# Transposing feed-forward features with VectorE blocks and SBUF-to-SBUF transfers in place of TensorE

## The chip, the cores and the metric

The kernel runs on one core of one Trainium2 chip. The metric is device microseconds for one execution. The profile is of one such execution; in it PE is TensorE's matmuls, PEld its weight loads, DVE is VectorE, ACT is ScalarE, SP is SyncE, whose queue issues nearly all transfers. L404 is line 404 of the kernel before.

## The reference

The computation is one layer of an encoder on 256 tokens of width 2048, all in float32. The change touches only the channel sub-layer, a SwiGLU feed-forward network with 5632 inner features:

```python
h = h + rms_norm(mixed, g_mix_post[i])
fn = rms_norm(h, g_ffn_pre[i])
ff = (jax.nn.silu(fn @ w_ffn_gate[i]) * (fn @ w_ffn_up[i])) @ w_ffn_down[i]
h = h + rms_norm(ff, g_ffn_post[i])
```

Before it comes a mixing sub-layer (input projection, neighbourhood attention, a gated recurrence, output projection), after it a per-layer embedding gated by one more 2048x2048 projection.

## The kernel before

Tokens are in two tiles `t` of 128 (`NT` = 2). Every large product reads its weight matrix in tiles of 256x512 numbers (512 KB): SP loads one into `wr` (L337), ACT copies it, rounded to a shorter format, into `wh` (L360), DVE writes what the rounding left off into `wl` (L370), and TensorE forms three products per 128 rows and per token tile (L404 to L406): high by high, high by low, low by high. One weight tile is thus 12 matmuls of 512 columns. There are four `wr` buffers and four pairs `wh`/`wl`.

The inner features come in eleven pieces of 512, `f` = 0 to 10, in three parts: pieces 0 to 3, 4 to 7 and 8 to 10. For each piece, 8 weight tiles of `w_ffn_gate` and 8 of `w_ffn_up` are multiplied. `gate_post` puts the gate half through SiLU on ACT into `mid` (L1200); `up_post` multiplies the up half into it on DVE (L1212). The result `e` has tokens on the partitions. The down product needs the features there, so `up_post` has TensorE transpose `e` in 128x128 blocks, four blocks at a time, into a PSUM bank `tr` (`transposed`, L260), and `split` turns `tr` into a high half (ACT, L241) and a low half (DVE, L243), named `mid0h` and `mid0l` in the first part. After the pieces of a part come its 512-wide column blocks of the down product, 32 weight tiles of `w_ffn_down` (24 in the last part), which read those halves.

The order on every engine is fixed when the kernel is built. A planner keeps an estimated clock for ACT, DVE, PE and the transfers. Small tasks are generators: each `yield act(...)`, `yield dve(...)`, `yield dma(...)` names an engine and an estimated cost, and the planner places it among the rest. TensorE's main order of matmuls comes from the sequence of segments; other tasks are fitted around it. Each engine, and SP's queue, then works through its list strictly in order.

Of the kernel before, what the change touches and what calls it, by code (L numbers as in the profile page):

```python
# [10 lines left out]
F32 = mybir.dt.float32  # L11
# [5 lines left out]
P = 128  # L17
S = 256
NT = S // P
# [8 lines left out]
N = 512  # L28
# [20 lines left out]
W_BUFS = 4  # L49
R_BUFS = 4  # L50
SM_BUFS = 4
# [5 lines left out]
class Event:  # L57


    t = None  # L60
# [124 lines left out]
def act(n, tables=COPY, take=None, give=None):  # L185
    return ("act", 0.15 + 0.00082 * n, tables, take, give)


def dve(n, take=None, give=None):
    return ("dve", 0.08 + 0.00104 * n, None, take, give)  # L190


def pe(cost, take=None, give=None):
    return ("pe", cost, None, take, give)


def dma(kb, take=None):
    return ("dma", kb / 340.0, None, take, None)
# [3 lines left out]
def layer(ctx: ExitStack, tc: tile.TileContext, a: dict, out: bass.AP):  # L202
    nc = tc.nc
# [1 line left out]
    wp = ctx.enter_context(tc.tile_pool(name="wp", bufs=W_BUFS))  # L205
    at = ctx.enter_context(tc.tile_pool(name="at", bufs=1))
    ps = ctx.enter_context(tc.tile_pool(name="ps", bufs=4, space=bass.MemoryType.PSUM))
    plan = Plan(wr=R_BUFS, w=W_BUFS, sm=SM_BUFS, ev=1, mid=2, bt=2)

    def f32(t):  # L210
        return t.bitcast(F32)

    def bank(name):
        return ps.tile([P, 2, S], F32, tag="sm", name=name, bufs=SM_BUFS)
# [23 lines left out]
    def split(hi, lo, src, n, give=None):  # L238

        yield act(n)  # L240
        nc.scalar.copy(hi, src)  # L241
        yield dve(n, give=give)
        nc.vector.tensor_tensor(out=lo, in0=src, in1=f32(hi), op=ALU.subtract)  # L243
# [9 lines left out]
    def transposed(e, b0):  # L253

        yield pe(0.44, take="sm")
        tr = bank("tr")
        for b in range(2):
            for t in range(NT):
                sl = slice((b0 + b) * P, (b0 + b + 1) * P)
                nc.tensor.transpose(tr[:, b, t * P : (t + 1) * P], e[:, t, sl], ident)  # L260
        return tr
# [13 lines left out]
    def done(event):  # L275
        event.t = plan.now
# [35 lines left out]
    def seg(chunk, w, n0, lhs, ks, first=True, last=True, after=None):  # L312
        s = (chunk, lhs, ks, first, last, after, len(tiles))
        for k, _ in ks:
            tiles.append((w, k, n0))
        segs.append(s)
# [658 lines left out]
    KS = [(k, k) for k in range(0, KD, 2)]  # L975
# [13 lines left out]
    t2 = {}  # L989

    def open_p2():
        for e in mixT.ev:
            plan.reach(e)
        p1_ctx.close()
        rs = ctx.enter_context(tc.tile_pool(name="rs", bufs=1))
        t2["pool"] = rs
        for n in ("h", "mg", "ple"):
            t2[n] = rs.tile([P, NT, D], F32, name=n)
        t2["pTh"] = rs.tile([P, 2, S], F32R, name="pTh")
        t2["pTl"] = rs.tile([P, 2, S], F32R, name="pTl")  # L1000
        t2["pw"] = rs.tile([P, 2, S], F32, name="pw")
        plan.add(load_p2(), plan.clk["pe"])

    pT = Act(2)
# [9 lines left out]
    def load_p2():  # L1014
        yield from load_gain("g_mix_post")
        done(ev_gain["mix"])
        yield dma(256)
        here = Event()
        nc.sync.dma_start(t2["pw"], a["pT"].rearrange("(k p) s -> p k s", p=P))
        done(here)  # L1020
        for t in range(NT):
            yield dma(1024)
            nc.sync.dma_start(t2["h"][:, t, :], a["x"][t * P : (t + 1) * P, :])
        done(ev_h)
        yield here
        yield from split(t2["pTh"], t2["pTl"], t2["pw"], 2 * S)
        pT.blocks(t2["pTh"], t2["pTl"], 0, 2)
        pT.pair(0)
# [131 lines left out]
    hF = Act()  # L1160
    rstd_f, ev_rf = small("rstd_f"), Event()

    def sub_post(sub, c, add=False, after=None):
        def post(ch):
            if c == 3:
                plan.add(after(), plan.now)
            yield from sub.chunk(c, ch, add)
        return post

    def after_mix():  # L1170
# [3 lines left out]
    A_KS = [(k, k) for k in range(0, 8, 2)]  # L1174
    ch = [
        Chunk(sub_post(mix, c, after=after_mix), None if c else open_p2) for c in range(4)
    ]
    for c in range(2):
# [14 lines left out]
    def gate_post(f):  # L1193
        def post(ch):
            yield ev_rf
            for t in range(NT):
                yield act(N, SILU, take=None if t else "mid")
                if t == 0:
                    es[f] = t2["pool"].tile([P, NT, N], F32, tag="mid", name="mid", bufs=2)
                nc.scalar.activation(  # L1200
                    es[f][:, t, :], ch.accs[t], AF.Silu, scale=rstd_f[:, t : t + 1]
                )
            done(ch.free)
        return post

    def up_post(f, mid, kk0, g):
        def post(ch):
            yield g.free
            e = es.pop(f)
            for t in range(NT):  # L1210
                yield dve(N)
                nc.vector.scalar_tensor_tensor(  # L1212
                    out=e[:, t, :], in0=ch.accs[t], scalar=rstd_f[:, t : t + 1], in1=e[:, t, :],
                    op0=ALU.mult, op1=ALU.mult,
                )
            done(ch.free)
            for b in range(0, 4, 2):
                tr = yield from transposed(e, b)
                if b == 2:
                    plan.free["mid"].append(plan.now)  # L1220
                kk = kk0 + b
                i, j = divmod(kk, 8)
                hi, lo = mid.tiles(i)
                yield from split(hi[:, j : j + 2, :], lo[:, j : j + 2, :], tr, 2 * S, give="sm")
                mid.pair(kk)
        return post

# [12 lines left out]
    def down_post(part, c):  # L1240
        def post(ch):
            sl = slice(c * N, (c + 1) * N)
            mg = t2["mg"]
            for t in range(NT):
                if part == 0:
                    yield act(N)
                    nc.scalar.copy(mg[:, t, sl], ch.accs[t])
                else:
                    yield dve(N)
                    nc.vector.tensor_tensor(  # L1250
                        out=mg[:, t, sl], in0=ch.accs[t], in1=mg[:, t, sl], op=ALU.add
                    )
            done(ch.free)
        return post
# [5 lines left out]
    for part, (f0, f1) in enumerate(parts):  # L1260
        mid = Mid(f"mid{part}")
        for f in range(f0, f1):
            g = Chunk(gate_post(f))
            seg(g, "w_ffn_gate", f * N, hF, KS)
            seg(Chunk(up_post(f, mid, (f - f0) * 4, g)), "w_ffn_up", f * N, hF, KS)
        for c in range(4):
            last = part == len(parts) - 1
            post = sub_post(ffn, c, True, after_ffn) if last else down_post(part, c)
            seg(Chunk(post), "w_ffn_down", c * N, mid,
                [(f0 * 4 + k, k) for k in range(0, (f1 - f0) * 4, 2)],  # L1270
                after=(lambda: load_sqrt()) if last and c == 3 else None)
# [13 lines left out]
    def load_sqrt():  # L1285
        plan.add(preload(AF.Sqrt, SQRT), plan.clk["pe"])
# [155 lines left out]
```

## Time and profile before

| | |
|---|---|
| median of 3 runs | 1195.0 us (1194.61 to 1195.26) |
| profiled execution, whole time | 1195.0 us |
| its span, first to last instruction | 1193.2 us |
| mean granted TensorE clock | 0.997 |
| PE / DVE / ACT busy share | 99% / 58% / 53% |
| share of the 16 DMA engines used by SP's queue | 59.3% |

A busy share says how full an engine is on average, not whether it sets the end; for that one reads the chain that ended last. A group's line gives `output<-inputs`, the shape, how often it ran, its busy time and its mean, and what it waited for. A DMA line gives the time from issue to landing, so its wait in the queue is in it. Matmuls overlap: one is recorded with about 390 ns, while the next starts some 227 ns after it, so what a matmul costs is read from starts.

### The profile page before, as it was taken

To read this page: it belongs to the slowest core of one execution; us is meant where nothing else is said; L and a number is where in the kernel's file an instruction comes from. 1 tells how busy PE (TensorE), PEld (TensorE's weight loads), DVE (VectorE), ACT (ScalarE), POOL (GpSimd) and SP (SyncE) were. 2 spreads that over 40 slices of the span, in tenths; PEclk is the share of its full clock that TensorE was granted. 3 is DMA by queue.
4 is the path that set the end of the run, shared out by engine and by line. 5 is a ranking of instruction groups with operands and counts; after the bars stand their busy time and mean duration, and the time that the engine had idled before them with its cause. 6 is when DMAs were issued, how large, how long until landed. Compare 5 with 4: busy or idle time off the path is not lost.

```text
span 1193.2 us, 14281 instructions
## 1 busy us (share of the span) xinstructions
PE 1180.8 (99%) x5396; PEld 978.0 (82%) x5396; DVE 697.7 (58%) x822; ACT 632.8 (53%) x836; POOL 1.2 (0%) x11
## 2 busy tenths in 40 slices
PE   9999999999999999999999999999999999999996
PEld 6888888888888888888888888888888888888885
DVE  6667967877557544544444544545454544657664
ACT  6777787866457444444444444444334444446753
POOL 0000000000000000000000000000000000000000
PEclk9999999999999999999999999999999999999998
DMA  9665555465856565565556565555665556565661
GB/s 339 228 207 191 171 186 189 153 192 188 301 192 197 193 194 190 186 191 190 194 195 194 182 197 185 189 196 181 194 193 194 191 181 194 175 209 177 221 220 71
DMA packets 69653, 233.01 MB, mean 195 GB/s; under 512 B 7376, under 2 KB 14160, under 8 KB 68944
## 3 DMA queue, kind: packets, MB, share of 16 engines
q1 hardware_dynamic: 69440, 232.03, 59.3%
q8 instruction: 42, 0.69, 0.2%
q14 instruction: 27, 0.22, 0.1%
q10 hardware_dynamic: 144, 0.08, 0.0%
HBM read 229.98 MB, written 2.10 MB: 195 GB/s over the span
## 4 chain that ended last, share of the span: by engine, by line
PE 98%; DMA 1%; DVE 1%; ACT 0%; SPq 0%; DVEq 0%; issue 0%
PE acc L406 31%; PE acc L405 31%; PE acc L404 31%; PE tr L260 2%; DMA wr<-in_w_in 1%; PE pg L265 0%; PE pg L266 0%; PE pg L264 0%; DVE wl L370 0%; DVE h L1328 0%; PE po L265 0%; PE po L266 0%; PE po L264 0%; PE sc L265 0%; PE sc L266 0%; PE sc L264 0%
## 5 line engine op out<-in xcount | busy, mean ns | idle before, releaser
L370 DVE TENSOR_TENSOR wl<-wr,wh 128x1024 fp32r<-128x1024 f32 x406 | 494.6, 1223 | 382.7 <-ACT wh L360 382.4
L360 ACT CAST wh<-wr 128x1024 fp32r<-128x1024 f32 x406 | 426.2, 1052 | 469.8 <-PE acc L406 450.5
L404 PE MATMUL acc<-wh,hT_mix_hi 128*128 128x512 f32 x704 | 275.8, 392 | 0.0
L406 PE MATMUL acc<-wh,hT_mix_lo 128*128 128x512 f32 x704 | 274.3, 390 | 0.3 <-DVE hT_mix_lo L249 0.3
L405 PE MATMUL acc<-wl,hT_mix_hi 128*128 128x512 f32 x704 | 274.0, 389 | 0.0
L406 PEld LDWEIGHTS acc<-wh,hT_mix_lo 128*128 128x128 f32 x704 | 132.2, 188 | 28.4 <-DVE hT_mix_lo L249 0.9
L405 PEld LDWEIGHTS acc<-wl,hT_mix_hi 128*128 128x128 f32 x704 | 132.3, 188 | 26.8
L404 PEld LDWEIGHTS acc<-wh,hT_mix_hi 128*128 128x128 f32 x704 | 132.2, 188 | 26.7
L404 PE MATMUL acc<-wh,hT_hi 128*128 128x512 f32 x312 | 123.8, 397 | 0.0
L405 PE MATMUL acc<-wl,hT_hi 128*128 128x512 f32 x312 | 121.9, 391 | 0.4 <-DVE wl L370 0.4
L406 PE MATMUL acc<-wh,hT_lo 128*128 128x512 f32 x312 | 121.9, 391 | 0.0
L405 PEld LDWEIGHTS acc<-wl,hT_hi 128*128 128x128 f32 x312 | 58.7, 188 | 12.8 <-DVE wl L370 1.5
L406 PEld LDWEIGHTS acc<-wh,hT_lo 128*128 128x128 f32 x312 | 58.6, 188 | 12.4
L404 PEld LDWEIGHTS acc<-wh,hT_hi 128*128 128x128 f32 x312 | 58.7, 188 | 11.4 <-ACT hT_hi L247 0.2
L404 PE MATMUL acc<-wh,mid0h 128*128 128x512 f32 x128 | 50.0, 390 | 0.0
L404 PE MATMUL acc<-wh,mid1h 128*128 128x512 f32 x128 | 50.0, 390 | 0.0
L406 PE MATMUL acc<-wh,mid0l 128*128 128x512 f32 x128 | 49.8, 389 | 0.0
L406 PE MATMUL acc<-wh,mid1l 128*128 128x512 f32 x128 | 49.8, 389 | 0.0
L405 PE MATMUL acc<-wl,mid0h 128*128 128x512 f32 x128 | 49.8, 389 | 0.0
L405 PE MATMUL acc<-wl,mid1h 128*128 128x512 f32 x128 | 49.8, 389 | 0.0
L404 PE MATMUL acc<-wh,hT_ffn_hi 128*128 128x512 f32 x112 | 44.2, 394 | 0.0
L406 PE MATMUL acc<-wh,hT_ffn_lo 128*128 128x512 f32 x112 | 43.7, 390 | 0.0
(236 smaller groups left out, 1330.3 us busy)
## 6 DMA issues: line engine op xcount, KB each, us to landing
wr<-in_w_ffn_gate SPq DMA_DIRECT2D x88, 512.0 KB, 4.1
wr<-in_w_ffn_up SPq DMA_DIRECT2D x88, 512.0 KB, 4.1
wr<-in_w_ffn_down SPq DMA_DIRECT2D x88, 512.0 KB, 4.2
wr<-in_w_in SPq DMA_DIRECT2D x79, 512.0 KB, 4.2
wr<-in_w_out SPq DMA_DIRECT2D x32, 512.0 KB, 4.5
wr<-in_w_ple_gate SPq DMA_DIRECT2D x32, 512.0 KB, 3.8
xn<-in_x SPq DMA_DIRECT2D x4, 512.0 KB, 6.9
bt<-in_bias SPq DMA_DIRECT2D x8, 256.0 KB, 3.5
```

The source lines that it names most:

```text
L260: nc.tensor.transpose(tr[:, b, t * P : (t + 1) * P], e[:, t, sl], ident)
L360: nc.scalar.copy(his[i][:, j, :], raws[i][:, j, :])
L370: nc.vector.tensor_tensor(out=los[i][:, j, :], in0=raws[i][:, j, :], in1=f32(his[i][:, j, :]), op=ALU.subtract,)
L404: nc.tensor.matmul(accs[t], hi[:, sl], wh[:, j, :], start=st, stop=False)
L405: nc.tensor.matmul(accs[t], hi[:, sl], wl[:, j, :], start=False, stop=False)
L406: nc.tensor.matmul(accs[t], lo[:, sl], wh[:, j, :], start=False, stop=sp)
```

## The change

In each part, all pieces but the last no longer go to TensorE for their transposition: 8 of the 11 pieces (`soon` is true only for `f` = 3, 7 and 10, which keep the old way). For those 8, DVE transposes every 32x32 block of `e` within itself, the blocks staying where they are, in one instruction, into a new buffer `m2`; then 16 transfers, SBUF to SBUF, move the blocks to their places in a second new buffer `mT`. Each takes 32 partitions to 32 partitions, 8 runs of 32 numbers (128 bytes) per partition, 32 KB in all. `split` then reads `mT` in place of `tr`. `m2` shares its memory with `pw`, a small input that is used up earlier. Both new buffers exist once.

```diff
-    plan = Plan(wr=R_BUFS, w=W_BUFS, sm=SM_BUFS, ev=1, mid=2, bt=2)
+    plan = Plan(wr=R_BUFS, w=W_BUFS, sm=SM_BUFS, ev=1, mid=2, bt=2, m2=1, mt=1)
...
-        t2["pw"] = rs.tile([P, 2, S], F32, name="pw")
+        pw = rs.tile([P, NT, N], F32, tag="m2", name="pw", bufs=1)
+        t2["pw"] = pw[:, 0, :].rearrange("p (k s) -> p k s", k=2)
...
+            if soon:
+                for b in range(0, 4, 2):
+                    tr = yield from transposed(e, b)
...
+                return
+            rs = t2["pool"]
+            yield dve(2 * N, take="m2", give="mid")
+            e2 = rs.tile([P, NT, N], F32, tag="m2", name="m2", bufs=1)
+            nc.vector.transpose(
+                out=e2.rearrange("p t n -> p (t n)"), in_=e.rearrange("p t n -> p (t n)")
+            )
+            src = e2.rearrange("p t (k j b) -> p t k j b", j=4, b=32)
+            mT = None
+            for i in range(4):
+                for j in range(4):
+                    yield dma(150, take=None if mT else "mt")
+                    if mT is None:
+                        mT = rs.tile([P, NT, 4, P], F32, tag="mt", name="mT", bufs=1)
+                    dst = mT.rearrange("p t k (i b) -> p t k i b", b=32)
+                    nc.sync.dma_start(
+                        dst[32 * j : 32 * j + 32, :, :, i, :],
+                        src[32 * i : 32 * i + 32, :, :, j, :],
+                    )
+            there = Event()
+            done(there)
+            plan.free["m2"].append(plan.now)
+            yield there
             for b in range(0, 4, 2):
-                tr = yield from transposed(e, b)
-                if b == 2:
-                    plan.free["mid"].append(plan.now)
...
-                yield from split(hi[:, j : j + 2, :], lo[:, j : j + 2, :], tr, 2 * S, give="sm")
+                yield from split(
+                    *(x[:, j : j + 2, :].rearrange("p k (t q) -> p k t q", t=NT) for x in (hi, lo)),
+                    mT[:, :, b : b + 2, :].rearrange("p t k q -> p t k q"), 2 * S,
+                    give="mt" if b else None,
+                )
...
-            seg(Chunk(up_post(f, mid, (f - f0) * 4, g)), "w_ffn_up", f * N, hF, KS)
+            seg(Chunk(up_post(f, mid, (f - f0) * 4, g, f == f1 - 1)), "w_ffn_up", f * N, hF, KS)
```

On TensorE the built order loses 16 groups of four transposes (two for each of the 8 pieces) and is otherwise the same, instruction for instruction. On DVE one block transposition is added right behind the two multiplications of each of the 8 pieces. On SP the weight loads keep their order and the new transfers are put between them. Where the loads of the first pieces stand on SP's queue before (`x8` is eight in a row):

```order
L337 DMA wr<-in_w_ffn_gate 128x1024 x3
L337 DMA wr<-in_w_ffn_up 128x1024 x8
L337 DMA wr<-in_w_ffn_gate 128x1024 x8
L337 DMA wr<-in_w_ffn_up 128x1024 x8
L337 DMA wr<-in_w_ffn_gate 128x1024 x8
```

Now the eighth gate load of piece 1 has three transfers of piece 0 ahead of it; behind it and the first up load of piece 1 the queue goes on like this, to the last up load (`m_3537` is piece 0's `m2`):

```order
L1243 DMA mT<-m_3537 32x8x32
L337 DMA wr<-in_w_ffn_up 128x1024
L1243 DMA mT<-m_3537 32x8x32 x3
L337 DMA wr<-in_w_ffn_up 128x1024
L1243 DMA mT<-m_3537 32x8x32 x2
L337 DMA wr<-in_w_ffn_up 128x1024
L1243 DMA mT<-m_3537 32x8x32 x2
L337 DMA wr<-in_w_ffn_up 128x1024
L1243 DMA mT<-m_3537 32x8x32 x3
L337 DMA wr<-in_w_ffn_up 128x1024
L1243 DMA mT<-m_3537 32x8x32 x2
L337 DMA wr<-in_w_ffn_up 128x1024 x2
```

So the 16 transfers of a piece are spread over the loads of the next one; the last two stand behind the sixth up load.

ACT before, from the SiLU of piece 0 (`acc_3127`, `acc_3128`) to that of piece 1 (`acc_3518`, `acc_3519`):

```order
L1200 ACTIVATE mid<-acc_3127,rstd_f 128x512
L1200 ACTIVATE mid<-acc_3128,rstd_f 128x512
L360 CAST wh<-wr 128x1024 x9
L241 CAST mid0h_3543<-tr 128x512
L360 CAST wh<-wr 128x1024
L241 CAST mid0h_3543<-tr 128x512
L360 CAST wh<-wr 128x1024 x5
L1200 ACTIVATE mid<-acc_3518,rstd_f 128x512
L1200 ACTIVATE mid<-acc_3519,rstd_f 128x512
```

And the same stretch now, a little further:

```order
L1201 ACTIVATE mid<-acc_3127,rstd_f 128x512
L1201 ACTIVATE mid<-acc_3128,rstd_f 128x512
L360 CAST wh<-wr 128x1024 x15
L1201 ACTIVATE mid<-acc_3518,rstd_f 128x512
L1201 ACTIVATE mid<-acc_3519,rstd_f 128x512
L241 CAST mid0h_3683<-mT 128x512
L360 CAST wh<-wr 128x1024
L241 CAST mid0h_3683<-mT 128x512
L360 CAST wh<-wr 128x1024 x15
```

Piece 0's two copies of `split` have moved behind piece 1's SiLU, half a piece later, and the first waits for all 16 transfers. DVE's two L243 move with them.

More of the change, by code (lines that the diff above doesn't have):

```diff
@@ L1204, in gate_post, with up_post @@
         return post
-    def up_post(f, mid, kk0, g):
+    def up_post(f, mid, kk0, g, soon):
         def post(ch):
@@ L1216, in post @@
             done(ch.free)
+            if soon:
+                for b in range(0, 4, 2):
+                    tr = yield from transposed(e, b)
+                    if b == 2:
+                        plan.free["mid"].append(plan.now)
+                    i, j = divmod(kk0 + b, 8)
+                    hi, lo = mid.tiles(i)
+                    yield from split(hi[:, j : j + 2, :], lo[:, j : j + 2, :], tr, 2 * S, give="sm")
+                    mid.pair(kk0 + b)
+                return
[21 more added lines that the diff above has]
+            yield there
             for b in range(0, 4, 2):
-                tr = yield from transposed(e, b)
-                if b == 2:
-                    plan.free["mid"].append(plan.now)
                 kk = kk0 + b
@@ L1223, in post @@
                 hi, lo = mid.tiles(i)
-                yield from split(hi[:, j : j + 2, :], lo[:, j : j + 2, :], tr, 2 * S, give="sm")
+                yield from split(
+                    *(x[:, j : j + 2, :].rearrange("p k (t q) -> p k t q", t=NT) for x in (hi, lo)),
+                    mT[:, :, b : b + 2, :].rearrange("p t k q -> p k t q"), 2 * S,
+                    give="mt" if b else None,
+                )
                 mid.pair(kk)
```

## The prediction

> **What bounds the kernel.** I read the page's shares and its chain first, then the feed-forward stages by windows, then single instructions there.
>
> ```profile
> PE 1180.8 (99%) x5396; PEld 978.0 (82%) x5396; DVE 697.7 (58%) x822; ACT 632.8 (53%) x836; POOL 1.2 (0%) x11
> ...
> PE 98%; DMA 1%; DVE 1%; ACT 0%; SPq 0%; DVEq 0%; issue 0%
> ```
>
> The chain of what ended last lies on TensorE for 98%. The windows (engine busy time, then clock, DMA share and rate) cover the pieces of the first two parts:
>
> ```profile
> 381.00:560.00 179.00, 179.00 (x807) 148.30 (x806) 88.57 (x81) 79.13 (x84) 0.00 (x0) 1.00 0.60 194
> ...
> 646.00:825.00 179.00, 179.00 (x807) 148.30 (x806) 90.37 (x83) 76.13 (x80) 0.00 (x0) 1.00 0.59 190
> ```
>
> In both, PE is busy for all 179.00 us at full granted clock, with DVE and ACT about half idle and the DMA engines at 0.60. So an instruction removed from TensorE there shortens the run by its own cost, as long as weights keep coming; nothing else counts unless it starves TensorE.
>
> **What is removed.** The list of the instructions on the tile `mid` gives counts (duration min/median/max, in ns):
>
> ```profile
> L260 PE MATMUL tr<-ident,mid x88: 270/272/273, 404.8 to 1027.0; 128*128 128x128 f32 x88
> ```
>
> 88 are 8 per piece, so 8 pieces lose 64, in 16 groups of four. The 272 ns overlap with neighbours; the cost is read from starts, in the timeline around the first group (start, length, in us):
>
> ```profile
> 401.13 0.39 PE L406 MATMUL acc<-wh,hT_mix_lo 128*128 128x512 f32 x1
> ...
> 403.85 0.39 PE L406 MATMUL acc<-wh,hT_mix_lo 128*128 128x512 f32 x1
> ...
> 404.53 0.39 PE L406 MATMUL acc<-wh,hT_mix_lo 128*128 128x512 f32 x1
> 404.76 0.60 PE L260 MATMUL tr<-ident,mid 128*128 128x128 f32 x4
> 405.11 0.48 PE L404 MATMUL acc<-wh,hT_mix_hi 128*128 128x512 f32 x1
> ...
> 407.72 0.39 PE L406 MATMUL acc<-wh,hT_mix_lo 128*128 128x512 f32 x1
> ```
>
> From 401.13 to 403.85 are 12 matmul steps in 2.72 us, 0.227 each, one weight tile. From 404.53 to 407.72 are again 12 steps, with the group among them: 3.19 us. A group costs 3.19 - 2.72 = 0.47 us, so 16 x 0.47 = 7.5 us go, all on the path: about 0.94 per piece.
>
> The Trainium skill (VectorE: DVE Perf Modes, "The three transpose paths") gives TensorE 390 ns for a 128x128 transposition, on bf16. By that figure the estimate would be 64 x 0.39 = 25 us and 1170 us. The trace differs: 0.47 / 4 = 0.12 us of TensorE's time each, so 7.5 stands.
>
> **What is added on DVE.** One block transposition of 128x1024 per piece, a form the trace lacks. The nearest row has the same shape with two inputs; the timeline shows the place:
>
> ```profile
> L370 DVE TENSOR_TENSOR wl<-wr,wh x406: 1198/1225/1227, 12.5 to 1165.4; 128x1024 fp32r<-128x1024 f32 x136
> ```
>
> ```profile
> 401.75 1.40 DVE L1212 SCALAR_TENSOR_TENSOR mid<-acc,rstd_f,mid 128x512 f32<-128x512 f32 x2
> 403.32 1.23 DVE L370 TENSOR_TENSOR wl<-wr,wh 128x1024 fp32r<-128x1024 f32 x1 [0.17 <-ACT wh L360]
> ```
>
> I take 1.2 us, between 0.6 (half, one input) and 2.5 (double). It runs from 403.15 to 404.4 and pushes one `wl` back by 1.1 us. What covers that is the stock of split weights:
>
> ```profile
> 402.24 1.06 ACT L360 CAST wh<-wr 128x1024 fp32r<-128x1024 f32 x1 [1.67 <-PE acc L406]
> 404.96 1.05 ACT L360 CAST wh<-wr 128x1024 fp32r<-128x1024 f32 x1 [1.67 <-PE acc L406]
> ...
> 414.06 1.05 ACT L360 CAST wh<-wr 128x1024 fp32r<-128x1024 f32 x1 [1.67 <-PE acc L406]
> ```
>
> ACT's cast waits until TensorE gives a pair back, so at that moment three of four pairs are ahead: 3 x 2.72 = 8.2 us of work. Cast and `wl` take 2.4 (402.24 to 404.55). The reserve is about 5.7 us at each tile, restored within a tile or two because ACT needs 1.05 and DVE 1.23 of every 2.72. The added 1.1 us costs nothing; without the cover it would cost 8 x 1.1 = 9 us.
>
> **What moves in `split`.** The high and low copies read SBUF, not PSUM: rows of that kind are as long as those now.
>
> ```profile
> L241 ACT CAST mid0h<-tr x8: 580/580/580, 405.9 to 542.5; 128x512 fp32r<-128x512 f32 x8
> ...
> L241 ACT CAST attn_hi<-attnT x3: 613/614/620, 261.5 to 264.7; 128x512 fp32r<-128x512 f32 x3
> ```
>
> Some 0.03 us more, on an idle ACT: nothing. The down product that reads them is at least one whole piece (44 us) away.
>
> **What is added on SP's queue and the DMA engines.** Per piece 16 transfers; the nearest are the gate weights of the recurrence, 256 runs of 512 bytes each, against 256 of 128 here:
>
> ```profile
> L650 SPq DMA_DIRECT2D av<-in_w_rg_a x8: 379/450/470, 47.4 to 182.5; - x8
> ...
> DMA to landing us min/median/max: 2.1/3.8/5.2
> ```
>
> Issue: 16 x 0.45 = 7.2 us of SP per piece, beside 16 weight loads; SP can issue while it waits for nothing else. In the densest tile it adds 3 x 0.45 = 1.35 of 2.72 us. Data: the window in which those runs were nearly alone (packets, MB, share of 16 engines), and one over all of the first part's pieces:
>
> ```profile
> q1 hardware_dynamic: 600, 0.31, 105.5%
> ```
>
> ```profile
> q1 hardware_dynamic: 9542, 34.76, 59.7%
> ...
> wr<-in_w_ffn_up SPq DMA_DIRECT2D x26, 512.0 KB, 3.8
> wr<-in_w_ffn_gate SPq DMA_DIRECT2D x24, 512.0 KB, 4.2
> wr<-in_w_ffn_down SPq DMA_DIRECT2D x15, 512.0 KB, 4.2
> ```
>
> The first window is 1 us: 1.055 x 16 / 600 = 28 ns per packet. The second is 180 us: 65 loads, one per 2.77 us, each 0.597 x 180 / 65 = 1.65 us of every engine, so 1.12 us are free per tile. 16 x 256 runs over 16 engines are 256 packets an engine. I take 28 ns, as packet count is nearest: 7.2 us a piece, within the 9.0 free in the eight tiles over which they are spread. The ends are 7 ns (by bytes, a quarter) and 180 ns (as the mean packet of the second window, 0.597 x 16 x 180 / 9542). Loads are put back by at most the three transfers ahead of them and the wait for DVE:
>
> ```profile
> 386.33 18.57 SPq L337 DMA_DIRECT2D wr<-in_w_ffn_gate  x8
> 408.41 19.77 SPq L337 DMA_DIRECT2D wr<-in_w_ffn_up  x8
> ```
>
> The eighth gate load left at about 404.6; now it follows the block transposition (404.4) and three issues: 405.8, 1.2 us late. A `wr` given back at 404.55 and landed 4.2 later, at 408.8, is cast at 414.06: 5 us of reserve ahead of ACT's own. Nothing, again.
>
> **The new wait.** ACT's first copy from `mT` has all further casts behind it. The sixth up load went at 408.41 + 5 x 2.78 = 422.3, the last transfer 0.33 + 0.45 later, at 423.1, landing at 426.9 by the median 3.8 (428.3 by 5.2).
>
> ```profile
> 424.26 1.37 ACT L1200 ACTIVATE mid<-acc,rstd_f 128x512 f32<-128x512 f32 x2 [0.99 <-PE acc L406]
> 425.53 1.04 ACT L360 CAST wh<-wr 128x1024 fp32r<-128x1024 f32 x1
> ```
>
> ACT arrives at 425.6, waits 1.3 (2.7), copies 0.6, and casts at 427.5, 2.0 us late (3.4), out of a reserve of 5.7. Both sides come about 0.9 earlier than before; the difference holds. It costs nothing up to a landing of 3.8 + 3.7 = 7.5 us.
>
> **Sum.** -7.5 on TensorE, 0 for the rest. The profiled execution took 1195.0 us (span 1193.2), equal to the median: 1195.0 - 7.5 = 1187.5 us.
>
> **Rivals.**
> 1. Slower: the 128-byte packets are dear. Free engine time per piece is 16 x 1.12 = 17.9 us; at 256 packets that is 70 ns each. Above it the weight loads set the pace of the 8 pieces: 1187.5 + 8 x (0.256p - 17.9), p in ns. The gain is gone at 74 ns; at the 180 ns end it is 1413 us. For it: no run so short is in the trace, and its packets differ in reading SBUF. Against: 512-byte packets took 28.
> 2. Less gain: the transfers land late and ACT's copy blocks the casts. 1187.5 + 8 x (landing - 7.5). Rows give 5.2 at most for the like transfers, with four in flight, not 16 among loads. At 8.1 us it is 1192.3, within the noise at 8.2 to 8.7, slower beyond.
> 3. The DVE transposition is many times longer than 1.2 us. At 5.8 us the reserve is used up, at 6.7 the gain; around that lies no change. Half-idle DVE speaks against it, the missing form for it.
> 4. The blocks are moved number by number. 131,072 packets a piece, 8192 an engine, at 28 ns 229 us; with the loads' 26, 256 us in place of 44: 8 x 211 = 1690 us more, about 2880 us. The order lists the runs as 32 numbers, so hardly. Here stands the trap of the Trainium skill (VectorE: DVE Perf Modes, "The three transpose paths"): a plain copy that transposes by access-pattern strides is 19 times slower than a crossbar transposition when the innermost destination stride is large. Its condition is not met as the order writes the runs; no run here shows it.
>
> That the change doesn't do what it says is excluded for TensorE: the built order has the 64 fewer.
>
> **How the numbers follow.** Forecast 0.73. Rival 2 0.13: 0.08 still faster, 0.03 same, 0.02 slower. Rival 1 0.09, rival 4 0.01, both slower. Rival 3 0.04: half same, half slower. So faster 0.81, same 0.05, slower 0.14, with 0.2% (2.4 us) about what can be told from no change. The range starts at 1186.5, the forecast less a little more than the runs' spread of 0.65, and ends at 1192.6, where rival 2's gain falls to 0.2%: 0.81 in it.
>
> **What would show it.** TensorE without idle time in the pieces and 64 fewer L260; a piece 43.5 us long; DVE's new row near 1.2 us; ACT waiting 1 to 3 us for `mT` once a piece; small packets under 70 ns. Wrong would be: TensorE waiting for `wl` in the middle of pieces 1 to 3, with casts behind `mT`, or behind loads that land late.

## The result

The changed kernel took 1187.72 us (median, 1187.51 to 1188.32) against 1195.13 us before, a ratio of 0.9936 with a 95% interval of 0.9925 to 0.9947: 7.4 us less. Forecast were 1187.5 us and 7.5 us less, in a range of 1186.5 to 1192.6. One of the twelve executions of the run with everything added, below, took 3099.92 us, for a cause that no trace here shows; all other executions agree with the rest of their kernel within 0.6%.

Line numbers in the changed kernel differ a little: L1201 is the SiLU, L1214 the multiplication, L1232 the block transposition, L1243 the transfers.

The page of the changed kernel, shares and chain:

```profile
PE 1173.1 (99%) x5332; PEld 971.5 (82%) x5332; DVE 706.6 (60%) x830; ACT 633.5 (53%) x836; POOL 1.2 (0%) x11
...
PE 98%; DMA 1%; DVE 1%; ACT 0%; SPq 0%; DVEq 0%; issue 0%
```

TensorE has 64 instructions and 7.7 us of recorded work less; the chain is as much its own as before. The same two windows, and the list of what TensorE waited for in the whole run (total us, times, longest):

```profile
381.00:560.00 179.00, 179.00 (x795) 148.27 (x794) 92.89 (x84) 80.94 (x85) 0.00 (x0) 1.00 0.67 205
646.00:825.00 179.00, 179.00 (x795) 148.30 (x794) 94.56 (x88) 77.46 (x80) 0.00 (x0) 1.00 0.66 201
```

```profile
PE acc L386 <- DMA wr<-in_w_in: 1.7, 2, 1.3
PE warm L1408 <- POOL ones L225: 1.1, 1, 1.1
PE acc L405 <- DVE wl L370: 0.4, 1, 0.4
PE acc L406 <- DVE hT_mix_lo L249: 0.3, 1, 0.3
```

TensorE is still busy throughout, at full clock, and none of its waits is in a piece. (The windows do not fit the pieces exactly: each starts behind the gate product of its part's first piece and holds some 25 us of the down product. TensorE is busy in all of it, so the reading stands.) What grew is DVE (by 4 us per window) and the DMA share (0.60 to 0.67), both off the path.

The profiled execution took 1188.06 us with a span of 1186.3, so the two spans differ by 6.9 us, not 7.4. The missing part is in the first microseconds, before the change has done anything. The timeline of TensorE there, before and after (start, length, wait):

```profile
9.52 3.67 PE L386 MATMUL acc<-wr,xs 128*128 128x512 f32 x8 [0.46 <-DVE la L552]
```

```profile
10.22 3.67 PE L386 MATMUL acc<-wr,xs 128*128 128x512 f32 x8 [1.28 <-DMA wr<-in_w_in]
```

TensorE started these eight matmuls 0.70 us later in this execution, waiting for a weight load. 6.9 + 0.7 = 7.6 us is what the pieces gave, 16 groups at 0.47.

### The profile page after: what moved, and what is told of

The parts are those of the page before. It is cut to its first block, busy times and chain, and to the rows that moved or that the text cites. A ratio compares the mean times of both kernels' runs of the same rounds, so it can differ in the third digit from the quotient of the medians.

```text
span 1186.3 us, 14329 instructions
## 1 busy us (share of the span) xinstructions
PE 1173.1 (99%) x5332; PEld 971.5 (82%) x5332; DVE 706.6 (60%) x830; ACT 633.5 (53%) x836; POOL 1.2 (0%) x11
## 4 chain that ended last, share of the span: by engine, by line
PE 98%; DMA 1%; DVE 1%; ACT 0%; SPq 0%; DVEq 0%; issue 0%
PE acc L406 31%; PE acc L405 31%; PE acc L404 31%; PE tr L260 2%; DMA wr<-in_w_in 1%; PE pg L265 0%; PE pg L266 0%; PE pg L264 0%; DVE wl L370 0%; DVE h L1363 0%; PE po L265 0%; PE po L266 0%; PE po L264 0%; PE sc L265 0%; PE sc L266 0%; PE sc L264 0%
## 5 line engine op out<-in xcount | busy, mean ns | idle before, releaser
L405 PEld LDWEIGHTS acc<-wl,hT_hi 128*128 128x128 f32 x312 | 58.7, 188 | 12.7 <-DVE wl L370 1.4
```

What stands on the lines that cost most here:

```text
L405: nc.tensor.matmul(accs[t], hi[:, sl], wl[:, j, :], start=False, stop=False)
```

## The experiments

Each edit is against the changed kernel; `...` marks lines left out. Ratios are to the kernel before, run on the same chip as the experiment (its medians there were 1195.50 to 1196.19 us), with their 95% interval.

**The transfers left out.**

```diff
-            src = e2.rearrange(...)
-            (the 16 transfers)
+            mT = e2.rearrange("p t (k q) -> p t k q", q=P)
```

> The 16 SBUF-to-SBUF transfers of each of the 8 pieces are left out; split reads the block-transposed buffer directly, so the features are not in their places. DVE's block transposition stays, TensorE's 64 transposes stay away. Theory (the change saves TensorE's own time, everything else lies under cover): 1187.7 us, the same as the changed kernel within 1 us. Rival (the transfers cost TensorE something, by queue or memory traffic, and the saving is larger than 16 x 0.47 us): 1183 to 1186 us.

Measured: 1188.38 us, 0.9938 (0.9926 to 0.995), the changed kernel's 0.9936 over again. The transfers cost TensorE nothing that can be measured.

**Everything added, nothing taken away.**

```diff
...
-            if soon:
+            if not soon:
+                plan.add(also(e), plan.now)   # block transposition, transfers, copies from mT into a scratch tile
+            if True:
                 (TensorE's transposes, as before)
```

> All 11 pieces are transposed by TensorE as before, and the 8 pieces get the block transposition, the 16 transfers and the copies from mT on ACT and DVE on top, their results unused. Theory (added work is hidden): 1195.1 us, the time before, within 1 us. Rival (added work costs, and the removed transposes saved more than they show): 1196 to 1200 us.

Measured: 1195.93 us, 1.0001 (0.9992 to 1.001); the kernel before took 1195.62 us beside it. With the run above it splits the change: the saving is that of the 64 transposes, and what was added is under cover, to within the 1 us or so that these intervals can tell.

**The block transposition repeated, 4 and 7 times.**

```diff
+            for _ in range(4):    # 7 in the other
                 nc.vector.transpose(...)
```

> The block transposition is done 4 times in a row (4 x 1.25 = 5.0 us on DVE instead of 1.25), with the order on every engine otherwise unchanged. Theory (the stock of split weights covers 5.7 us at this place): no change, 1187.7 us within 1 us. Rival (the cover is much smaller, 3 us or less): 8 x 2 = 16 us more, 1204 us.

> The block transposition is done 7 times (8.7 us on DVE). Theory (cover 5.7 to 6 us, then TensorE waits for wl): 2.7 to 3 us per piece, 8 times, 1209 to 1212 us, with TensorE's wait behind each of the 8 transpositions. Rival (the cover is far larger, since eight tiles are held in raw and split form): no change, 1188 us.

Measured: four times 1187.83 us, 0.9935 (0.9923 to 0.9948), no change. Seven times 1222.14 us, 1.0225 (1.0212 to 1.0238), some 10 us beyond the expectation. The reserve lies between the two, as read. DVE's order around the first of the seven-fold transpositions, TensorE's waits, then three windows around the second wait and, for contrast, two around the end of the first:

```profile
403.99 8.92 DVE L1233 STREAM_TRANSPOSE m<-mid 128x1024 f32<-128x1024 f32 x7
412.84 4.59 DVE L370 TENSOR_TENSOR wl<-wr,wh 128x1024 fp32r<-128x1024 f32 x4
```

```profile
PE acc L405 <- DVE wl L370: 21.9, 9, 2.7
```

```profile
457.00:460.00 3.00, 0.89 (x4) 0.39 (x3) 2.96 (x3) 1.04 (x1) 0.00 (x0) 1.00 0.00 0
460.00:463.50 3.50, 2.93 (x7) 2.35 (x8) 3.50 (x4) 0.00 (x0) 0.00 (x0) 0.51 0.39 75
463.50:466.00 2.50, 2.50 (x12) 2.06 (x12) 0.42 (x1) 0.03 (x1) 0.00 (x0) 1.00 0.99 304
```

```profile
412.00:414.00 2.00, 0.00 (x0) 0.00 (x0) 2.00 (x3) 0.25 (x1) 0.00 (x0) 1.00 0.00 0
414.00:416.00 2.00, 1.93 (x8) 1.61 (x9) 2.00 (x3) 0.00 (x0) 0.00 (x0) 1.00 0.30 49
```

The waits are the 2.7 us expected, eight times 2.7 (the ninth, 0.4, stands in the changed kernel's list as well). ACT's cast for the first `wl` behind the transposition had ended at 404.11, so that `wl` was 8.7 us late; less TensorE's wait of 2.7 this makes a reserve of 6.0 us. But behind the second wait the granted clock (third number from the end, 0.51) is half for 3.4 us: 7 matmuls start in 3.5 us, where 12 start in 2.5 afterwards. Behind the first it is not. The trace's clock record has six such spells of 3.41 us after the eight waits; each loses up to half its length, 6 x 1.7 = 10 us at most. 21.5 + 10 = 31.5 us, and the profiled execution is 32.8 us longer than the changed kernel's. So a wait of TensorE can cost more than its length.

**All 11 pieces, nothing else changed.**

```diff
-... up_post(f, mid, (f - f0) * 4, g, f == f1 - 1)
+... up_post(f, mid, (f - f0) * 4, g, False)
```

> All 11 pieces take the new way, with nothing else changed. Theory: TensorE saves 3 x 0.94 us more, but the down product needs the last piece's features 6 tiles (16 us; 4 tiles, 11 us, in the last part) after the up product, and they come after about 26 to 28 us: TensorE waits 8 to 12 us at each of the three parts, 1210 to 1220 us. Rival (the wait is short, because the transfers go as fast as the queue allows): 1185 to 1190 us.

Measured: 1217.38 us, 1.0179 (1.0164 to 1.0195). TensorE's waits:

```profile
PE acc L404 <- ACT mid2h L241: 9.5, 1, 9.5
PE acc L404 <- ACT mid0h L241: 8.3, 1, 8.3
PE acc L404 <- ACT mid1h L241: 7.9, 1, 7.9
```

25.7 us of waiting, one per part, at the first down product that needs the last piece. The clock record shows TensorE at half clock for 4.0, 5.9 and 3.0 us after them, 6.5 us lost. 25.7 + 6.5 - 2.8 saved = 29.4; measured are 29.7 more than the changed kernel. The theory's range held, though it had no term for the clock. Here the path from `e` to `mid` is the critical one: TensorE's transposition is short, the new way takes some 25 us.

**Two more pieces, needed later.** In the first two parts all pieces go the new way, and the down product holds two column blocks open:

```diff
...
+        held = () if last else (0, 1)
+        for c in held:
+            seg(down[c], "w_ffn_down", c * N, mid, early, last=False)
+        for c in held:
+            seg(down[c], "w_ffn_down", c * N, mid, late, first=False)
+        for c in range(len(held), 4):
...
```

> In the first two parts the last piece takes the new way as well (10 of 11 pieces), and the down product's first two column blocks are taken first without that piece's features and then finished with them, so that they are needed 12 weight tiles (33 us) after the up product's end and not 6 (16 us). Part three as in the changed kernel. Theory: two more pieces save 2 x 0.94 us of TensorE and no wait appears, since the copies from mT end some 28 us after the up product: 1185.8 us. Rival (a wait at the first down product, or the reordering itself costs): 1188 us or more.

Measured: 1185.76 us (1185.47 to 1186.2), 0.9918 (0.9903 to 0.9933). The forecast 1185.8 held; its trace has no wait of TensorE on `mid`. It is ahead of both kernels; its runs do not overlap those of the changed one, though they are from another chip (before took 1195.50 there).

**The same in the last part too.** The loop above with `held = (0, 1)` in every part, and 11 pieces moved.

> As the kernel with 10 pieces moved, but the last part's last piece takes the new way too, with its first two column blocks held open in the same manner: its features are needed 8 tiles, 21.8 us, after the up product's end. Theory: they come after about 26 us, as in the changed kernel (402.4 to 428.4), so TensorE waits some 4 us once, runs 3.41 us at half clock after it, and saves 0.94: 1190.8 us. Rival (the planner brings the transfers early enough): 1184.8 us.

Measured: 1189.00 us (1187.61 to 1190.73), 0.9944 (0.9929 to 0.9959). Its wait and the clock behind it:

```profile
PE acc L404 <- ACT mid2h L241: 2.7, 1, 2.7
```

```profile
1036.00:1046.00 10.00, 9.71 (x30) 7.72 (x31) 3.89 (x5) 2.86 (x5) 0.00 (x0) 0.67 0.28 82
1046.00:1052.00 6.00, 6.00 (x29) 4.95 (x28) 4.78 (x6) 3.86 (x8) 0.00 (x0) 1.00 0.41 144
```

The wait is 2.7 us, not 4. ACT's copies there, for a multiplication on DVE that began at 1011.38:

```profile
1035.62 1.14 ACT L241 CAST mid2h<-mT 128x512 fp32r<-128x512 f32 x2 [0.94 <-DMA mT<-m]
```

TensorE went on at 1036.3, with the first high half, 24.9 us after the multiplication's start; I had counted to the low half, 26. The ten microseconds after it ran at 0.67 of the clock, 3 us lost. 2.7 + 3 - 0.94 = 4.8, and the profiled execution is 5.0 us longer than that of the kernel with 10 pieces moved. The medians differ by 3.2, since the loss varies: the four executions took 1190.73, 1189.38, 1188.62 and 1187.61 us at mean granted clocks of 0.994, 0.997, 0.997 and 0.998. The direction was right, the two sizes were not.

**Shorter runs, the same bytes.** Each run of 32 numbers becomes 2, 4 or 8 runs of 16, 8 or 4 numbers; the edit for 8, in which the slices of each transfer follow the new form:

```diff
-            src = e2.rearrange("p t (k j b) -> p t k j b", j=4, b=32)
+            src = e2.rearrange("p t (h j b) -> p (t h) j b", j=4, b=8)
...
-                    dst = mT.rearrange("p t k (i b) -> p t k i b", b=32)
+                    dst = mT.rearrange("p t k (h i b) -> p (t k h) i b", i=4, b=8)
...
```

> Each transfer moves the same bytes in runs of 8 numbers (32 bytes) instead of 32; the numbers land in other places of mT. 1024 packets per engine and piece in place of 256. Theory (a packet takes about 10 ns, 10.5 us per piece, 17.9 us are free): 1187.7 us within 1.5 us. Rival (a short packet or its descriptor takes over 17 ns here): 1195 us or more.

> The same with runs of 4 numbers (16 bytes): 2048 packets per engine and piece. Theory (about 10 ns each: 20 us of every DMA engine per piece beside 26 us for the weights, against a piece of 43.5 us): the weight loads set the pace, 2 to 3.5 us more for each of the 8 pieces, 1203 to 1215 us. Rival (something other than engine time, such as issuing, limits short runs): far more, 1250 us and up; or (weights run on reserves): 1188 us.

Measured: 32 bytes 1213.75 us, 1.0159 (1.013 to 1.0187); 16 bytes 1299.02 us, 1.0869 (1.0853 to 1.0886). Both far over the theory; with 16 bytes the rival's 1250 us and up came. ACT's timeline with 32 bytes, and the DMA queue in a 3 us window in which three transfers were issued (all packets, then SP's queue as a share of 16 engines):

```profile
424.37 1.37 ACT L1201 ACTIVATE mid<-acc,rstd_f 128x512 f32<-128x512 f32 x2 [0.99 <-PE acc L406]
432.42 0.62 ACT L241 CAST mid0h<-mT 128x512 fp32r<-128x512 f32 x1 [6.68 <-DMA mT<-m]
```

```profile
DMA packets 2830, 0.75 MB, mean 249 GB/s; under 512 B 2668, under 2 KB 2668, under 8 KB 2830
...
q1 hardware_dynamic: 2830, 0.75, 114.7%
```

The packets were not dearer. The 162 long ones take 162 x 0.2 = 32 of the window's 1.147 x 16 x 3 = 55 us of engine time, so the short ones took some 8.5 ns; the mean of all 131,072 in the trace is 8.3. 1024 of them are 8.5 us per engine and piece, which with eight loads (13.2) makes 21.7 of the 21.8 us of eight tiles. But the engines were not full all that time: in the five windows from 405 to 430 us, which end at 411, 416, 421, 426 and 430, their share was 0.63, 0.94, 0.78, 0.86 and 0.74. The delay shows earlier, in SP's issues. Four rows of the changed kernel, then the same four with 32 bytes:

```profile
411.09 1.90 SPq L1243 DMA_DIRECT2D mT<-m  x3
...
416.15 0.33 SPq L337 DMA_DIRECT2D wr<-in_w_ffn_up  x1
...
419.24 1.89 SPq L1243 DMA_DIRECT2D mT<-m  x3
...
421.96 1.24 SPq L1243 DMA_DIRECT2D mT<-m  x2
```

```profile
411.45 4.17 SPq L1243 DMA_DIRECT2D mT<-m  x3
...
418.07 2.03 SPq L337 DMA_DIRECT2D wr<-in_w_ffn_up  x1
...
423.24 3.42 SPq L1243 DMA_DIRECT2D mT<-m  x3
...
427.41 1.29 SPq L1243 DMA_DIRECT2D mT<-m  x2
```

Issues take longer, and the last two transfers go 5.45 us later, about as much as the first copy from `mT` (432.42 against 427.04). What holds an issue back, packets still queued or something in the issuing itself, was not separated; the 16-byte run's rival, a limit other than engine time, stays open.

I had let lateness be shared by the whole stock; but it falls all on the first copy from `mT`, and ACT stood 6.7 us there, with 0.6 for the copy 1.6 more than the reserve of 5.7. Eight times 1.6 are 13 us, and TensorE's listed waits come to 14. So the 17.9 us of free engine time per piece were no measure of what fits: 8.5 us of short packets between eight loads were already too many. With 16 bytes (2048 x 7.8 ns = 16 us) ACT waits 15 us. The profiled execution with 32 bytes is 23.3 us longer than the changed kernel's: 14 are those waits, some 5 are three spells of 3.41 us at half clock, and the rest was not traced to a row.

> The transfers in runs of 16 numbers (64 bytes): 512 packets per engine and piece; the numbers land in other places of mT. In the 32-byte kernel a packet took 8.3 ns but the last transfer landed 5 us later and ACT waited 6.7 us for mT, past its reserve. Theory (the lateness comes with the number of runs, and half of it still fits the reserve): no change against the changed kernel, 1187.7 us within 1 us, with ACT's wait for mT between 2 and 4 us. Rival (anything under 128 bytes is slow): 1195 us or more.

Measured: 1187.60 us, 0.9932 (0.9915 to 0.9948), and ACT's first wait for `mT`:

```profile
426.67 0.62 ACT L241 CAST mid0h<-mT 128x512 fp32r<-128x512 f32 x1 [2.23 <-DMA mT<-m]
```

So runs of 64 bytes are still free here, runs of 32 are not.

## Why the prediction was right

**The saving** was 16 x 0.47 us, read from starts, and that mechanism is what the runs show: a piece takes 43.5 us, where it took 44.5. The list of the instructions on `mid` has 24 of 88 left:

```profile
L260 PE MATMUL tr<-ident,mid x24: 270/272/273, 536.0 to 1020.2; 128*128 128x128 f32 x24
```

**DVE's transposition** was put at 1.2 us; the row, and its place in the timeline:

```profile
L1232 DVE STREAM_TRANSPOSE m<-mid x8: 1246/1246/1247, 403.9 to 971.5; 128x1024 f32<-128x1024 f32 x8
```

```profile
403.87 1.25 DVE L1232 STREAM_TRANSPOSE m<-mid 128x1024 f32<-128x1024 f32 x1
405.04 1.18 DVE L370 TENSOR_TENSOR wl<-wr,wh 128x1024 fp32r<-128x1024 f32 x1
406.73 1.22 DVE L370 TENSOR_TENSOR wl<-wr,wh 128x1024 fp32r<-128x1024 f32 x1 [0.51 <-ACT wh L360]
```

One `wl` is pushed back, the next already waits for ACT again. Four in a row (5.1 us) cost nothing, seven did and gave a reserve of 6.0 us: the 5.7 are right, and rival 3 lay far off.

**Packets** were taken at 28 ns, between 7 and 180. SP's queue from 381 to 560 us, to be held against the row of before (380 to 560):

```profile
q1 hardware_dynamic: 22650, 36.49, 66.4%
...
wr<-in_w_ffn_down SPq DMA_DIRECT2D x16, 512.0 KB, 4.3
mT<-m SPq DMA_DIRECT2D x48, 32.0 KB, 3.3
```

0.664 x 16 x 179 - 0.597 x 16 x 180 = 182 us more, 26 of it for one load more by count of issues; 156 us over some 13,000 packets are 12 ns, and the mean of all 32,768 packets of 128 bytes in the trace is 12.7. The term was mis-sized by a factor of two, on the safe side, and that was luck. At the assumed 28 ns the transfers would have taken 7.2 us of every engine per piece, between the run with 64 bytes (512 x 10.6 ns = 5.4 us, free) and that with 32 (8.5 us, 26 us slower), so that they fit would not have been sure. The Trainium skill (DMA: Bandwidth & Descriptors, "Why small descriptors are slow (HBM only)") says that SBUF-to-SBUF transfers don't suffer the penalty of small descriptors. By the byte this trace shows a penalty all the same: 12.7 ns for 128 bytes are 0.10 ns a byte, against 0.05 for the 512-byte packets from HBM (27.5 ns) and for the 4096-byte ones (199 ns).

**Issue and landing** were taken from the recurrence's loads, 0.45 us and 3.8. They were

```profile
L1243 SPq DMA_DIRECT2D mT<-m x128: 585/604/1604, 405.1 to 990.3; - x128
...
DMA to landing us min/median/max: 1.9/3.4/5.8
```

0.60 and 3.4; that the two errors nearly cancel is luck. **The new wait** was forecast as 1.3 us (up to 2.7) and is there:

```profile
424.01 1.37 ACT L1201 ACTIVATE mid<-acc,rstd_f 128x512 f32<-128x512 f32 x2 [0.99 <-PE acc L406]
427.04 0.62 ACT L241 CAST mid0h<-mT 128x512 fp32r<-128x512 f32 x1 [1.67 <-DMA mT<-m]
427.57 1.05 ACT L360 CAST wh<-wr 128x1024 fp32r<-128x1024 f32 x1
```

Over the eight pieces ACT's waits for `mT` come to 9.7 us, 1.2 each.

**The rivals.** Rival 2 did not come, since 1.67 us is within the reserve; but its mechanism is the one that set in with 32 bytes, where TensorE waited for the casts behind ACT's copy. Rival 1's threshold of 70 ns was wrong: it let the transfers use a whole piece, where the order puts them between eight loads, with 9.0 us free, or 9.0 / 256 = 35 ns. Even that is no safe bound, since the 8.5 us of the 32-byte run were too many; whether fewer and dearer packets would do the same, no run shows. Its price had no term for the clock. At 12.7 ns neither mattered. Rival 4 was excluded by the order; the run with 4 numbers at a time is the nearest to it, 111 us slower than the change.

## What to carry to other kernels

Where TensorE is busy without a break, a transposition can be taken off it at its full cost in starts, not in recorded duration, if its result has time: here some 25 us from the block transposition to the copies, against a lead of 44. Before such a move, find the one in-order engine that will wait for the slow path and compare that wait with the stock of finished work ahead of TensorE; the reserve, not the average load, decides. The last piece before a consumer stays on the short path, or the consumer is reordered to need it later, which gave some 2 us more here.

## What was not expected of the hardware

A pause of TensorE of 2.7 us was enough, in six of eight cases, to halve its granted clock for 3.41 us, which adds up to 1.7 us to the pause; pauses of 8 to 9.5 us were followed by 3 to 6 us at half clock, and one more of 2.7 us by 6 us. The Trainium skill (TensorE: Matmul & The Clock Gate, "Part 1: The HAM clock gate") puts the drop after an idle window of about 3.4 us; the trace shows it after shorter pauses.

The clock record also says which pauses. Within an execution all half-clock spells begin whole multiples of 3.413 us apart, and they last 3.41, 6.83, 10.24 or, in the 16-byte run, 13.65 us: the clock changes on a fixed grid. With seven transpositions, the two pauses without a spell (from 411.39 and from 960.93) lay across a line of the grid, 0.9 us before it and 1.8 behind it. Of the other six, and of the 2.7 us pause with 11 pieces moved and two held open, at least 2.1 us fell into one interval, and half clock began at the end of that interval. So of two equal pauses one can be dearer than the other by where it falls.

Packets became only a little cheaper as the runs shrank: the means in the traces are 12.7, 10.6, 8.3 and 7.8 ns at 128, 64, 32 and 16 bytes. At these lengths the cost of a run is mostly per packet; an eighth of the bytes still took three fifths of the time.
